# Splitting a recurrent layer's weights one stage early, into DRAM scratch

## The chip, the cores and the metric

One core of one Trainium2 chip runs the whole program. The metric is device time in microseconds (us) of one launch, the median of several runs. A profile shows one execution on the same chip; its span and its own time stand in the table below.

## The reference, cut to what matters

Two decoder layers over 512 tokens of 1024 channels, in float32. Layer 0 is attention, then a squared-ReLU MLP. Layer 1 is an RWKV-7 recurrent mixer, then another MLP. A final norm closes it. The recurrent mixer and the MLP:

```python
h = rmsnorm(h)
xx = shift(h) - h
xr, xw, xk, xv, xa, xg = [h + xx * mu[i] for i in range(6)]
r, k, v = xr @ w_r, xk @ w_k, xv @ w_v                  # 1024 x 1024 each
w = f(w0 + tanh(xw @ w1) @ w2)                          # rank 64
a = sigmoid(a0 + (xa @ a1) @ a2)                        # rank 64
g = sigmoid(xg @ g1) @ g2                               # rank 160
y = scan over 512 tokens of a 64 x 64 state per head, 16 heads
out = (groupnorm(y) + bonus(r, k, v)) * g @ w_o         # 1024 x 1024
mlp(h) = square(relu(h @ W1)) @ W2                      # W1 1024 x 4096
```

## The kernel before, in words

**Products in three passes.** A float32 operand x is split into a high half hi = x cast to fp32r and a low half lo = x - hi. A product is three TensorE passes, hi*hi, hi*lo and lo*hi (`mm3`, L187 to L190). So each weight chunk has to be loaded (SyncE issues a DMA into `wraw`, L177), cast by ScalarE into `whi` (L179), and subtracted by VectorE into `wlo` (L181) before TensorE may read it. `wraw` has three buffers, `whi` and `wlo` two each. A chunk is 128 x 2 x 512 elements, 512 KB, and feeds 24 matmuls of 128x128 by 512 columns in `gemm_group`.

**Order.** Outside of the scan a scheduler at build time orders the instructions of each engine. It places an instruction as soon as, by its own reckoning, the operands and the buffer are there; the order in the program decides between two that are ready. On the chip each engine, and each engine's DMA queue, then runs in that fixed order. In the scan the order of TensorE, ScalarE, VectorE and GpSimd is written out by hand (class `InOrder`); only the DMA issues are still placed by the scheduler.

**The stages of interest.** (1) The MLP of layer 0, here *MLP0*: 32 chunks of W1, 32 of W2, TensorE all the time. (2) The *LoRA stage* of the recurrent layer (`rwkv_layer`, L757 to about L960). `mix` makes the six inputs: per channel tile VectorE computes `mt` (L799), ScalarE casts it to `xh` (L804), and `xl` = mt - xh is made by GpSimd, or by VectorE for odd tiles of all but the first mix (`XLA`, L806). For the first mix, `xk`, VectorE also makes `h` and `xx` for each tile (L795, L797). `project` multiplies by half of w_k or w_r in four chunks; `wa_weights` and `g_weights` load and split the LoRA weights (L819 to L844, L902); `wa_first`, `wa_second`, `g_first`, `g_second` multiply. Results go to DRAM scratch through `spill`, issued from ScalarE's queue (L768), out of five buffers `sp`. (3) The *scan*: 16 units of work on 128 tokens by 4 heads. Beside them `beside` and `project_o` run the products by w_v, half of w_r, and w_o. Their 28 chunks come from `chunks`: the DMA at L1510, then quarter by quarter ScalarE's cast and GpSimd's subtraction (L1525, L1526; where the hand-written order is on, all lines read L149). SyncE also issues the scan's own small transfers, among them `kb` (L1125 to L1140), which TensorE transposes (`tkb`).

Of the kernel before, what the change touches and what calls it, by code (L numbers as in the profile page):

```python
# [10 lines left out]
F32 = mybir.dt.float32  # L11
# [55 lines left out]
XLA = 63  # L67
# [89 lines left out]
class Builder:  # L157
    def __init__(self, tc, A, out):
        self.tc, self.nc, self.A, self.out = tc, tc.nc, A, out
        self.uid = 0  # L160
        self.xq = None
        self.late = 0
        self.summed = None
# [21 lines left out]

    def mm3(self, ps, lh, ll, rh, rl, start, stop):
# [14 lines left out]
    def gemm_group(self, w, row0, nk, c0, xh, xl, evac, token_major=False, kc=2, prep=None, chunk=None,  # L201
                   banks=None, meanwhile=None):
# [4 lines left out]
        for kk in range(0, nk, kc):  # L207
            wh, wl = (chunk or self.wchunk)(w, row0 + kk, c0, kc)
            if prep is not None:
                for k in range(kc):  # L210
                    prep(kk + k)
            if kk == nk - kc and meanwhile is not None:
                meanwhile()
            for m in range(4):
                for k in range(kc):
                    a = kk + k
                    ms = slice(m * P, (m + 1) * P)
                    st, sp = a == 0, a == nk - 1
                    if token_major:
                        self.mm3(banks[m], xh[a][:, ms], xl[a][:, ms], wh[:, k, :], wl[:, k, :], st, sp)  # L220
                    else:
                        self.mm3(banks[m], wh[:, k, ms], wl[:, k, ms], xh[a], xl[a], st, sp)
                if kk + kc == nk:
                    evac(m, banks[m])

# [531 lines left out]
    def rwkv_layer(self):  # L757
        tc, nc, A = self.tc, self.nc, self.A
        W = {n: A["rwkv_" + n][0] for n in ("w_r", "w_k", "w_v", "w_o", "w0", "w1", "w2", "a0", "a1", "a2", "g1", "g2")}
# [7 lines left out]
        def spill(name, t, b, hf):  # L767
            nc.scalar.dma_start(scr[name][b * P:(b + 1) * P, hf * 512:(hf + 1) * 512], t)  # L768

        with ExitStack() as ctx:  # L770
# [38 lines left out]
            def raw(shape):  # L809
                return self.wp.tile(list(shape), F32, tag="wraw", name=self.nm("wraw"), bufs=3)  # L810
# [5 lines left out]
            def pair(src, tag, shape, bufs=1):  # L816
                hi, lo = small(tag + "h", shape, bufs), small(tag + "l", shape, bufs)
                nc.scalar.copy(hi, src)
                nc.vector.tensor_tensor(lo, src, hi, op=ALU.subtract)  # L819
                return hi, lo  # L820
# [7 lines left out]
            def wa_weights(w1, w2, w0):  # L828
                r1 = raw([P, KT, P])
                for o in (0, HD):  # L830
                    nc.sync.dma_start(r1[:, :, o:o + HD], w1.rearrange("(k p) c -> p k c", p=P))
                first = pair(r1, "l1", [P, KT, P])
                r2, bias = raw([P, D]), raw([P, D])
                nc.sync.dma_start(r2[0:HD], w2)
                nc.sync.dma_start(r2[HD:], w2)
                nc.sync.dma_start(bias[HD:HD + 1], w0.unsqueeze(0))
                nc.sync.dma_start(bias[96:97], w0.unsqueeze(0))
                hi, lo = small("l2h", [P, D]), small("l2l", [P, D])
                nc.scalar.copy(hi, r2)
                nc.vector.tensor_tensor(lo[0:HD], r2[0:HD], hi[0:HD], op=ALU.subtract)  # L840
                nc.vector.tensor_scalar(lo[HD:], r2[HD:], 0.0, None, op0=ALU.mult)
                nc.scalar.copy(lo[HD:HD + 1], bias[HD:HD + 1])
                nc.scalar.copy(lo[96:97], bias[96:97])
                nc.vector.tensor_tensor(lo[96:97], bias[96:97], lo[96:97], op=ALU.subtract)  # L844
                return first, (hi, lo)

            def wa_first(x, w, func):
# [5 lines left out]
                nc.vector.tensor_scalar(s2[HD:], f[HD:], 0.0, 1.0, op0=ALU.mult, op1=ALU.add)  # L853
# [18 lines left out]
            def project(w, x, hf, evac, behind=None):  # L872
                self.gemm_group(w, 0, KT, hf * 512, *x, lambda m, ps: evac(m, hf, ps), token_major=True,
                                chunk=behind and (lambda *a: self.wchunk(*a, behind=behind)))
# [11 lines left out]
            def g_weights():  # L886
                r1 = raw([P, KT, P])
                nc.sync.dma_start(r1, W["g1"][:, 0:P].rearrange("(k p) c -> p k c", p=P))
                g1 = pair(r1, "l1", [P, KT, P])
                r1 = raw([P, KT, P])  # L890
                for o in range(0, 96, 32):
                    nc.sync.dma_start(r1[:, :, o:o + 32], W["g1"][:, P:].rearrange("(k p) c -> p k c", p=P))
                t1 = pair(r1[:, :, 0:96], "g1", [P, KT, 96])
                r2 = raw([P, D])
                nc.sync.dma_start(r2, W["g2"][0:P, :])
                g2 = pair(r2, "l2", [P, D])
                r3 = raw([P, D])
                for o in range(0, 96, 32):
                    nc.sync.dma_start(r3[o:o + 32], W["g2"][P:, :])
                t2 = small("gst", [P, D])  # L900
                nc.scalar.copy(t2[0:96], r3[0:96])
                nc.vector.tensor_tensor(t2[64:96], r3[64:96], t2[64:96], op=ALU.subtract)  # L902
                return g1, t1, g2, t2
# [26 lines left out]
            project(W["w_k"], xk, 0, spilled("k"), self.ended)  # L930
            ww = wa_weights(W["w1"], W["w2"], W["w0"])
# [3 lines left out]
            project(W["w_k"], xk, 1, spilled("k"))  # L935
            xa = mix(4, 0)
            wa = wa_weights(W["a1"], W["a2"], W["a0"])
# [3 lines left out]
            project(W["w_r"], xr, 0, spilled("r"))  # L941
# [11 lines left out]
            with ExitStack() as cx:  # L953
# [531 lines left out]
                def evac_r(q):  # L1485
                    def evac(bk, ps):
                        t = self.tmp.tile([P, S], F32, tag="sq", name=self.nm("sq"))
                        nc.scalar.copy(t, ps)
                        nc.scalar.dma_start(tokens("r", q, bk), t.rearrange("p (m c) -> p m c", m=2))
                    return evac  # L1490

                def evac_v(q):
                    def evac(bk, ps):
# [3 lines left out]
                        nc.scalar.dma_start(tokens("v", q, bk), t.rearrange("p (m c) -> p m c", m=2))  # L1497
# [5 lines left out]
                        nc.scalar.dma_start(tokens("vc", q, bk), t.rearrange("p (m c) -> p m c", m=2))  # L1503
# [3 lines left out]
                def loads(todo):  # L1507
                    for w, k0, kc, c0, nc_ in todo:
                        raw = self.wp.tile([P, kc, nc_], F32, tag="wraw", name=self.nm("wraw"), bufs=3)
                        nc.sync.dma_start(raw, w[k0 * P:(k0 + kc) * P, c0:c0 + nc_].rearrange("(k p) c -> p k c", p=P))  # L1510
                        yield raw

                def chunks(todo):

                    ahead = loads(todo)
                    raws = [next(ahead)]
                    for w, k0, kc, c0, nc_ in todo:
                        raws.append(next(ahead, None))
                        raw = raws.pop(0)
                        hi = self.wp.tile([P, kc, nc_], F32R, tag="whi", name=self.nm("whi"))  # L1520
                        lo = self.wp.tile([P, kc, nc_], F32R, tag="wlo", name=self.nm("wlo"))
                        parts = [t.rearrange("p k c -> p (k c)") for t in (raw, hi, lo)]
# [31 lines left out]
                def project_o(cg, ks, ts, banks=None, last=True):  # L1554
# [5 lines left out]
                    for k0 in ks:  # L1560
# [5 lines left out]
                        for m in range(4):  # L1566
# [6 lines left out]
                            if last and k0 == ks[-1] and m % 2:  # L1573
                                for z in (0, 1):
# [7 lines left out]
                order = [(W["w_v"], xv, evac_v, 0), (W["w_v"], xv, evac_v, 1), (W["w_r"], xr, evac_r, 2), (W["w_r"], xr, evac_r, 3),  # L1582
                         (W["w_v"], xv, evac_v, 2), (W["w_v"], xv, evac_v, 3)]
                first_o, whole_o = (0, 2), (0, 2, 4, 6)
                weights = chunks([(w, kk, 4, q * CW, CW) for w, x, e, q in order for kk in (0, 4)]
                                 + [(W["w_o"], k0, 2, cg * 512, 512) for ks in (first_o, whole_o) for cg in range(2) for k0 in ks]
                                 + [(W["w_o"], k0, 2, cg * 512, 512) for k0 in (4, 6) for cg in range(2)])
# [70 lines left out]
    def mlp(self, layer, meanwhile=None):  # L1658
        tc, nc, A = self.tc, self.nc, self.A
        W1, W2 = A["mlp_w1"][layer], A["mlp_w2"][layer]  # L1660
        with ExitStack() as ctx:
            mp = ctx.enter_context(tc.tile_pool(name=f"mp{layer}", bufs=1))
            mw = ctx.enter_context(tc.tile_pool(name=f"mw{layer}", bufs=3))
            xh, xl = self.xtiles()
# [4 lines left out]
            for gcol in range(DFF // 512):  # L1669
# [6 lines left out]
                self.gemm_group(W1, 0, KT, gcol * 512, xh, xl, evac, prep=prep_x if gcol == 0 else None)  # L1676
# [8 lines left out]
            for gcol in range(2):  # L1685
# [13 lines left out]
                self.gemm_group(W2, 0, DFF // P, gcol * 512, mh, ml, evac, prep=prep)  # L1699
# [50 lines left out]
```

## Time and profile before

| | |
|---|---|
| median of 3 runs | 1502.92 us (1500.44 to 1506.06) |
| profiled execution, its own time | 1504.68 us |
| profiled execution, span | 1502.9 us |
| TensorE busy | 1421.1 us, 95% |
| VectorE, ScalarE, GpSimd busy | 890.4, 703.0, 351.1 us |
| moved by DMA | 163.97 MB, 109 GB/s over the span |

The span is the time between the first and the last instruction. Busy times of TensorE (PE) are modelled ends of pipelined matmuls; a matmul at the lower granted clock counts as busy too. A line number is that of the kernel; in the hand-ordered part all lines read L149, and the tiles tell the operations apart. `SPq` and `ACTq` rows are DMA issues by SyncE and ScalarE.

### The profile page before, as it was taken

What the parts mean: (1) busy time and instruction counts of PE and PEld (TensorE: products, weight loads), DVE (VectorE), ACT (ScalarE), POOL (GpSimd) and SP (SyncE); (2) the same over time, 40 slices, a digit from 0 to 9 for tenths busy, and PEclk for the clock granted to TensorE, in tenths of its full rate; (3) what the DMA queues carried; (4) which work ended last, traced back from release to release, by engine and by line L of the source; (5) the groups of instructions that cost most, each with busy time, mean ns of one, the idle gap of its engine ahead of it and who ended that gap; (6) DMA issues with size and microseconds to landing.
All of it is one profiled execution on the core that took longest, in us unless ns stands there. A gap on an engine that the chain in (4) does not pass through costs nothing. (4 is left out here: it accounts for less than half of the span.)

```text
span 1502.9 us, 24530 instructions
## 1 busy us (share of the span) xinstructions
PE 1421.1 (95%) x9506; PEld 1174.4 (78%) x9506; DVE 890.4 (59%) x1531; ACT 703.0 (47%) x1426; POOL 351.1 (23%) x368
## 2 busy tenths in 40 slices
PE   8999999999999999888988999989989999999998
PEld 6777777878888888666767888867778888888887
DVE  6456687723344464597767778888756233444543
ACT  4346675423333343346535666666645233333533
POOL 5111100300000010152255455556554000000100
PEclk9999999999999999899989999989999999999999
DMA  5343231423333233325654355443234333332321
GB/s 200 88 109 93 84 88 47 111 84 98 99 98 98 93 123 95 111 85 168 188 177 132 98 156 152 128 133 105 78 92 113 94 99 98 98 99 95 92 95 69
DMA packets 119677, 163.97 MB, mean 109 GB/s; under 512 B 23036, under 2 KB 58404, under 8 KB 119560
## 3 DMA queue, kind: packets, MB, share of 16 engines
q1 hardware_dynamic: 106824, 145.62, 33.0%
q10 hardware_dynamic: 12736, 16.78, 3.1%
q8 instruction: 75, 1.23, 0.4%
q14 instruction: 42, 0.34, 0.1%
HBM read 133.00 MB, written 19.92 MB: 102 GB/s over the span
## 5 line engine op out<-in xcount | busy, mean ns | idle before, releaser
L181 DVE TENSOR_TENSOR wlo<-wraw,whi 128x1024 fp32r<-128x1024 f32 x172 | 221.0, 1285 | 251.8 <-ACT whi L179 251.6
L179 ACT CAST whi<-wraw 128x1024 fp32r<-128x1024 f32 x172 | 180.4, 1049 | 223.6 <-PE g L189 184.9
L190 PE MATMUL g<-xh,wlo 128*128 128x512 f32 x512 | 199.1, 390 | 0.7 <-DVE wlo L181 0.6
L188 PE MATMUL g<-xh,whi 128*128 128x512 f32 x512 | 199.4, 390 | 0.0
L189 PE MATMUL g<-xl,whi 128*128 128x512 f32 x512 | 199.3, 389 | 0.0
L188 PE MATMUL g<-mh,whi 128*128 128x512 f32 x512 | 199.2, 389 | 0.0
L189 PE MATMUL g<-ml,whi 128*128 128x512 f32 x512 | 199.2, 389 | 0.0
L190 PE MATMUL g<-mh,wlo 128*128 128x512 f32 x512 | 199.2, 389 | 0.0
L366 POOL TENSOR_TENSOR acc<-acc,sq 128x512 f32<-128x512 f32 x29 | 49.4, 1704 | 610.5 <-issue 436.6
L196 DVE TENSOR_TENSOR ml<-m,mh 128x512 fp32r<-128x512 f32 x128 | 87.9, 689 | 151.2 <-ACT mh L195 151.2
L195 ACT CAST mh<-m 128x512 fp32r<-128x512 f32 x128 | 78.9, 618 | 190.1 <-PE g L190 189.9
L190 PEld LDWEIGHTS g<-xh,wlo 128*128 128x128 f32 x512 | 96.1, 188 | 21.2 <-DVE wlo L181 1.6
L188 PEld LDWEIGHTS g<-mh,whi 128*128 128x128 f32 x512 | 96.1, 188 | 20.1
L188 PEld LDWEIGHTS g<-xh,whi 128*128 128x128 f32 x512 | 96.1, 188 | 20.0 <-ACT rb L372 0.2
L190 PEld LDWEIGHTS g<-mh,wlo 128*128 128x128 f32 x512 | 96.1, 188 | 19.9
L189 PEld LDWEIGHTS g<-xl,whi 128*128 128x128 f32 x512 | 96.1, 188 | 19.9
L189 PEld LDWEIGHTS g<-ml,whi 128*128 128x128 f32 x512 | 96.1, 188 | 19.8
L149 POOL TENSOR_TENSOR wlo<-wraw,whi 128x256 fp32r<-128x256 f32 x100 | 76.9, 773 | 120.0 <-ACT whi L149 116.1
L806 POOL TENSOR_TENSOR xl<-mt,xh 128x512 fp32r<-128x512 f32 x28 | 47.8, 1722 | 86.6 <-ACT xh L804 79.9
L149 PE MATMUL side<-whi,xh 128*128 128x256 f32 x192 | 63.8, 332 | 0.0
L149 PE MATMUL g<-xh,whi 128*128 128x512 f32 x128 | 51.9, 406 | 5.8 <-DVE Qka L494 3.1
L149 PE MATMUL side<-wlo,xh 128*128 128x256 f32 x192 | 55.5, 289 | 1.8 <-POOL wlo L149 1.7
(331 smaller groups left out, 3065.7 us busy)
## 6 DMA issues: line engine op xcount, KB each, us to landing
wraw<-in_mlp_w_dram SPq DMA_DIRECT2D x128, 512.0 KB
wraw<-in_attn_w_in_dram SPq DMA_DIRECT2D x24, 512.0 KB
wraw<-in_rwkv_w_o_dram SPq DMA_DIRECT2D x16, 512.0 KB
wraw<-in_attn_w_out_dram SPq DMA_DIRECT2D x8, 512.0 KB
wraw<-in_rwkv_w_k_dram SPq DMA_DIRECT2D x8, 512.0 KB
wraw<-in_rwkv_w_r_dram SPq DMA_DIRECT2D x8, 512.0 KB
wraw<-in_rwkv_w_v_dram SPq DMA_DIRECT2D x8, 512.0 KB
xt<-in_x_dram ACTq DMA_DIRECT2D x4, 512.0 KB
```

Of the source, the lines that this page charges most:

```text
L149: ins = op(*args, **kw)
L179: ins = [nc.scalar.copy(hi, raw)]
L181: ins.append((eng or nc.vector).tensor_tensor(lo, raw, hi, op=ALU.subtract))
L188: mm(ps, lh, rh, start=start, stop=False)
L189: mm(ps, lh, rl, start=False, stop=False)
L190: mm(ps, ll, rh, start=False, stop=stop)
L195: nc.scalar.copy(hi, src)
L196: nc.vector.tensor_tensor(lo, src, hi, op=ALU.subtract)
L366: nc.gpsimd.tensor_tensor(self.acc[0], self.acc[0], sq, op=ALU.add)
L806: eng.tensor_tensor(xl[k], t, xh[k], op=ALU.subtract)
```

## The change

During MLP0 a new function `split_ahead` makes 40 jobs. Each job loads a piece of the recurrent layer's weights, splits it (ScalarE cast, VectorE subtraction) and writes both halves to DRAM scratch. `gemm_group` gets a hook `between`, called behind each chunk of MLP0, from which the jobs are put into the program, about two jobs per three chunks from the third of 64 chunks to the 59th. Their tiles `sraw`, `shi`, `slo` have two buffers each. In the recurrent layer `kept` loads the two halves with two DMAs (into `whi` and `wlo`, or every third time into two of the three `wraw` buffers), in place of load, cast and subtraction. `chunks` does the same for the scan, and the casts and subtractions there go. Besides, all `xl` are made by VectorE; `spill` and the scan's result writes are issued by SyncE, not ScalarE; two constant fills move from VectorE to GpSimd; the first w_k chunks are no longer ordered behind the end of MLP0.

```diff
+    def split_ahead(self, sp):
+        def keep(key, *parts):
+            for n, t in enumerate(parts):
+                d = nc.dram_tensor(self.nm("wsplit"), list(t.shape), F32).ap()
+                nc.sync.dma_start(d, t.bitcast(F32))
+                self.parts.setdefault(key, []).append(d)
+        def halves(key, raw):
+            hi, lo = tile_("shi"), tile_("slo")
+            n = raw.shape[-1]
+            nc.scalar.copy(hi[:, :n], raw)
+            nc.vector.tensor_tensor(lo[:, :n], raw, hi[:, :n], op=ALU.subtract)
+            keep(key, hi[:, :n], lo[:, :n])
+        def chunk(name, k0, kc, c0, n):
+            def job():
+                raw = tile_("sraw", F32)
+                nc.sync.dma_start(raw.rearrange("p (k c) -> p k c", k=kc),
+                                  W[name][k0 * P:(k0 + kc) * P, c0:c0 + n].rearrange("(k p) c -> p k c", p=P))
+                halves((name, k0, c0), raw)
+            return job
...
+        jobs = project("w_k", 0) + [first("w1", 2, 0, HD), second("w2", "w0")] + project("w_k", 1)
+        jobs += [first("a1", 2, 0, HD), second("a2", "a0")] + project("w_r", 0)
+        jobs += [first("g1", 1, 0, P), first("g1", 3, P, 32), gate_second, gate_rest]
+        for name, q in (("w_v", 0), ("w_v", 1), ("w_r", 2), ("w_r", 3), ("w_v", 2), ("w_v", 3)):
+            jobs += beside(name, q)
+        for cg in range(2):
+            jobs += project("w_o", cg)
+    def kept(self, key, kc, n):
+        self.turn3 = (self.turn3 + 1) % 3
+        tags = ("wraw", "wraw") if self.turn3 == 0 else ("whi", "wlo")
+        out = []
+        for tag, d in zip(tags, self.parts[key]):
+            t = self.wp.tile([P, kc, n], F32R, tag=tag, name=self.nm(tag), **({"bufs": 3} if tag == "wraw" else {}))
+            self.nc.sync.dma_start(t.rearrange("p k c -> p (k c)").bitcast(F32), d)
+            out.append(t)
+        return out
...
         def spill(name, t, b, hf):
-            nc.scalar.dma_start(scr[name][b * P:(b + 1) * P, hf * 512:(hf + 1) * 512], t)
+            nc.sync.dma_start(scr[name][b * P:(b + 1) * P, hf * 512:(hf + 1) * 512], t)
...
-                    eng = nc.vector if not first and (XLA >> i & 1) and k % 2 else nc.gpsimd
-                    eng.tensor_tensor(xl[k], t, xh[k], op=ALU.subtract)
+                    nc.vector.tensor_tensor(xl[k], t, xh[k], op=ALU.subtract)
...
-            project(W["w_k"], xk, 0, spilled("k"), self.ended)
-            ww = wa_weights(W["w1"], W["w2"], W["w0"])
+            project("w_k", xk, 0, spilled("k"))
+            ww = wa_weights("w")
...
-                        for i in range(4):
-                            r, h, l = (t[:, i * 256:(i + 1) * 256] for t in parts)
-                            nc.scalar.copy(h, r)
-                            nc.gpsimd.tensor_tensor(l, r, h, op=ALU.subtract)
-                            yield (hi, lo) if i == 3 else None
+                    for name, k0, kc, c0, n in todo:
+                        yield self.kept((name, k0, c0), kc, n)
...
+            def between():
+                nonlocal slots
+                slots += 1
+                while todo and (len(jobs) - len(todo)) * (total - 6) < (slots - 2) * len(jobs):
+                    todo.pop(0)()
```

## Rows read from the trace of the kernel before

**Rows 1.** The page, part 1: busy us, share and instructions by engine.

```profile
PE 1421.1 (95%) x9506; PEld 1174.4 (78%) x9506; DVE 890.4 (59%) x1531; ACT 703.0 (47%) x1426; POOL 351.1 (23%) x368
```

**Rows 2.** Busy time by stretch: bounds, length, busy by engine, granted clock, DMA share, GB/s.

```profile
268.00:630.00 362.00, 358.64 (x1603) 297.10 (x1602) 165.23 (x192) 132.76 (x183) 24.70 (x16) 1.00 0.34 100
632.00:671.00 39.00, 29.40 (x108) 22.41 (x108) 38.37 (x39) 15.87 (x23) 19.18 (x10) 0.83 0.25 69
632.00:773.00 141.00, 115.74 (x452) 87.81 (x452) 115.32 (x123) 72.24 (x114) 49.31 (x31) 0.89 0.46 142
773.00:1140.00 367.00, 337.11 (x4375) 290.11 (x4376) 274.80 (x659) 218.62 (x618) 207.31 (x263) 0.97 0.42 125
```

**Rows 3.** TensorE's waits, 600 to 820 us: waiter, releaser, total, times, longest.

```profile
PE l L868 <- DVE ls L855: 6.5, 2, 5.5
PE g L188 <- ACT xh L804: 4.7, 1, 4.7
PE g L189 <- DVE wlo L181: 4.3, 1, 4.3
```

**Rows 4.** VectorE's groups, 632 to 773 us: count, busy, mean ns, idle before.

```profile
L799 DVE SCALAR_TENSOR_TENSOR mt<-xx,mu,h 128x512 f32<-128x512 f32 x48 | 39.7, 870 | 0.0
L806 DVE TENSOR_TENSOR xl<-mt,xh 128x512 fp32r<-128x512 f32 x20 | 22.5, 1129 | 2.3 <-ACT xh L804 2.1
L181 DVE TENSOR_TENSOR wlo<-wraw,whi 128x1024 fp32r<-128x1024 f32 x10 | 14.4, 1436 | 11.2 <-ACT whi L179 11.2
```

**Rows 5.** GpSimd's largest group, 632 to 773 us.

```profile
L806 POOL TENSOR_TENSOR xl<-mt,xh 128x512 fp32r<-128x512 f32 x28 | 47.8, 1722 | 86.6 <-ACT xh L804 79.9 <-ACT xh L802 6.7
```

**Rows 6.** VectorE in order of time, first mix: start, us, operation, count.

```profile
633.72 1.28 DVE L797 TENSOR_TENSOR xx<-h 128x512 f32<-128x512 f32 x2
634.92 1.41 DVE L799 SCALAR_TENSOR_TENSOR mt<-xx,mu,h 128x512 f32<-128x512 f32 x2
...
638.59 2.36 DVE L797 TENSOR_TENSOR xx<-h 128x512 f32<-128x512 f32 x2
```

**Rows 7.** ScalarE and VectorE in MLP0, around one chunk, in order of time.

```profile
401.43 1.06 ACT L179 CAST whi<-wraw 128x1024 fp32r<-128x1024 f32 x1 [4.38 <-PE g L189]
402.52 1.23 DVE L181 TENSOR_TENSOR wlo<-wraw,whi 128x1024 fp32r<-128x1024 f32 x1 [4.21 <-ACT whi L179]
406.87 1.06 ACT L179 CAST whi<-wraw 128x1024 fp32r<-128x1024 f32 x1 [0.54 <-PE g L189]
```

**Rows 8.** Results of the LoRA products: ScalarE's evictions and their DMA issues.

```profile
L882 ACT ACTIVATE sp<-g x12: 585/598/602, 666.9 to 744.0; 128x512 f32<-128x512 f32 x12
L768 ACTq DMA_DIRECT2D scr_k<-sp x8: 326/327/354, 667.5 to 706.4; - x8
```

**Rows 9.** SyncE's DMA issues in order of time, the recurrent layer's constants.

```profile
273.28 0.34 SPq L745 DMA_DIRECT2D tri<-in_c_tri_dram  x1
```

**Rows 10.** DMA: two queues of the page's part 3, and the densest stretch (columns of Rows 2).

```profile
q1 hardware_dynamic: 106824, 145.62, 33.0%
q10 hardware_dynamic: 12736, 16.78, 3.1%
...
773.00:790.00 17.00, 16.30 (x111) 15.31 (x112) 10.69 (x18) 5.45 (x13) 12.22 (x15) 0.90 0.75 243
```

**Rows 11.** The scan's weight splits, 773 to 1140 us, GpSimd and ScalarE groups.

```profile
L149 POOL TENSOR_TENSOR wlo<-wraw,whi 128x256 fp32r<-128x256 f32 x99 | 76.2, 774 | 120.0 <-ACT whi L149 116.1 <-POOL lw L149 1.2 <-issue 1.1
...
L149 ACT CAST whi<-wraw 128x256 fp32r<-128x256 f32 x95 | 38.4, 406 | 2.5 <-PE side L149 2.0
```

**Rows 12.** TensorE's longest waits in the scan, 773 to 1140 us.

```profile
PE pxs L149 <- DVE x L149: 4.3, 7, 0.9
...
PE side L149 <- POOL wlo L149: 1.7, 3, 1.1
```

**Rows 13.** A transfer of one unit and TensorE's first use, in order of time.

```profile
914.13 0.59 SPq L1140 DMA_DIRECT2D kb<-la  x1
916.86 0.60 PE L149 MATMUL tkb<-ident,kb 128*128 128x128 f32 x4
```

More of the change, by code (lines that the diff above doesn't have):

```diff
@@ L201, in gemm_group @@
     def gemm_group(self, w, row0, nk, c0, xh, xl, evac, token_major=False, kc=2, prep=None, chunk=None,
[L202 removed]
+                   banks=None, meanwhile=None, between=None):
         if banks is None:
@@ L224, in gemm_group @@
                     evac(m, banks[m])
+            if between is not None:
+                between()
     def gemm_stream(self, jobs, kc=2):
@@ L814, in small, with kept @@
                 return pool_.tile(list(shape), F32R, tag=tag, name=self.nm(tag), bufs=bufs)
[L816 to L820, printed above, removed]
+            def kept(key, tag, shape):
+                out = []
+                for d, z in zip(self.parts[key], "hl"):
+                    t = small(tag + z, shape)
+                    nc.sync.dma_start((t.rearrange("p k c -> p (k c)") if len(shape) == 3 else t).bitcast(F32), d)
+                    out.append(t)
+                return out
             def lora1(x, w, m):
@@ L826, in lora1, with wa_weights @@
                 return ps
[L828 to L845, printed above, removed]
+            def wa_weights(n):
+                return kept((n + "1", 0), "l1", [P, KT, P]), kept(n + "2", "l2", [P, D])
             def wa_first(x, w, func):
@@ L886, in g_weights @@
             def g_weights():
[L887 to L899, printed above, removed]
+                g1, t1, g2 = kept(("g1", 0), "l1", [P, KT, P]), kept(("g1", P), "g1", [P, KT, 96]), kept("g2", "l2", [P, D])
                 t2 = small("gst", [P, D])
-                nc.scalar.copy(t2[0:96], r3[0:96])
-                nc.vector.tensor_tensor(t2[64:96], r3[64:96], t2[64:96], op=ALU.subtract)
+                nc.sync.dma_start(t2[0:96].bitcast(F32), self.parts["gst"][0])
                 return g1, t1, g2, t2
@@ L1502, in evac @@
                         nc.vector.tensor_tensor(hv(t), hv(ps), m.unsqueeze(2).broadcast_to([P, 8, HD]), op=ALU.subtract)
-                        nc.scalar.dma_start(tokens("vc", q, bk), t.rearrange("p (m c) -> p m c", m=2))
+                        nc.sync.dma_start(tokens("vc", q, bk), t.rearrange("p (m c) -> p m c", m=2))
                     return evac
[L1507 to L1511, printed above, removed]
-                def chunks(todo):
[L1515 to L1522, printed above, removed]
-                        for i in range(4):
-                            r, h, l = (t[:, i * 256:(i + 1) * 256] for t in parts)
-                            nc.scalar.copy(h, r)
-                            nc.gpsimd.tensor_tensor(l, r, h, op=ALU.subtract)
-                            yield (hi, lo) if i == 3 else None
+                def chunks(todo):
+                    for name, k0, kc, c0, n in todo:
+                        yield self.kept((name, k0, c0), kc, n)
                 def product(dst, ops, opens, closes):
@@ L1698, in evac @@
                     self.ended = self.sq_accum(k), added
-                self.gemm_group(W2, 0, DFF // P, gcol * 512, mh, ml, evac, prep=prep)
+                self.gemm_group(W2, 0, DFF // P, gcol * 512, mh, ml, evac, prep=prep, between=between)
+            assert not todo
             self.rstd = self.rstd_tokens(-0.5, pn)
```

82 lines of the change are left out of this document (64 added, 18 removed).

## The prediction

> **What bounds the kernel now.** I read the busy shares first: TensorE is busy 95% of the span, no other engine more than 59% [rows 1]. So a gain can come only from TensorE's idle time and from matmuls run at the lower clock. The table by stretch says where these are [rows 2]. MLP0 (268 to 630 us) has TensorE busy 358.6 of 362 us at clock 1.00: nothing to win, only to lose. The LoRA stage (632 to 773 us) has 115.7 busy of 141 us at a mean granted clock of 0.89. The scan with its tail (773 to 1140 us) has 337.1 of 367 us at 0.97.
>
> How much of the LoRA stage is work? The code gives 448 matmuls of 512 columns: 12 projection chunks x 24 = 288, four LoRA first products x 24 = 96, the second products 2 x 16 + 32 = 64. The stretch counts 452, four of the scan's among them [rows 2]. At full clock one takes 5.44 / 24 = 0.227 us: the cast of the next chunk, which waits for TensorE each time, comes 5.44 us after the one before (401.43, 406.87) and a chunk is 24 matmuls [rows 7]. That is 101.5 us of work in 141 us.
>
> What holds it up? Over its first 39 us VectorE is busy 38.4 us and TensorE only 29.4 at clock 0.83 [rows 2]; TensorE's largest waits are for VectorE's LoRA operands, for `xh` and for a `wlo` [rows 3]. So VectorE sets the pace at first; later short waits and the clock that falls after them do.
>
> **The change part by part.**
>
> *LoRA stage, VectorE.* GpSimd's 28 `xl` take 47.8 us [rows 5], and while they run VectorE is slower: two `xx` took 1.28 us before the first of them and 2.36 us beside them [rows 6]. Over the stage 48 `mt` took 39.7 us where 48 x 0.705 = 33.8 was due, 20 `xl` 22.5 where the undisturbed two-input operation gives 20 x 0.64 = 12.8 [rows 4, 6]: 15.6 us lost in these two groups alone. The change removes that, and the `wlo` (14.4 us, [rows 4]), and adds 28 x 0.64 = 17.9 us. VectorE goes from 115.3 to at most 115.3 - 15.6 - 14.4 + 17.9 = 103 us, less the LoRA splits, which I don't price. The first mix now is `h`, `xx`, `mt`, `xl` per tile, 0.705 + 0.64 + 0.705 + 0.64 = 2.69 us, 21.5 us for eight. It starts at 632.4, so ends near 654; TensorE's first group needs 21.8 us and follows tile by tile, ending a chunk later, near 660. Before, its first eviction was at 666.9 [rows 8] and the last about 3 us later: some 10 us come from here. Behind it 101.5 - 21.8 = 79.7 us of matmuls remain, with VectorE no longer ahead of them. I leave 8 us for the waits of the second products on `ls` and the like, which the change does not touch [rows 3], and 5 us for the lower clock behind them: 660 + 79.7 + 13 = 753 instead of 773. **-20 us.** Ends: -35 us if only the first 4.4 us and the 101.5 us of work remain; the other end comes from the DMAs. The stage must move 12.6 MB of halves for the chunks, 7.5 MB for the LoRA weights, 9.4 MB of results, 2.1 MB of `h`: 31.6 MB. The densest 17 us of the trace moved 243 GB/s [rows 10]; at that rate 130 us, so -11 us; and if the wait for halves simply takes VectorE's place, 0. I take -20, since 243 GB/s came at a DMA share of only 0.75.
>
> *MLP0, the new work.* A job costs ScalarE one cast, VectorE one subtraction, as in the chunk rows 1.06 and 1.23 us [rows 7]. 40 jobs add 42 and 49 us to engines that are busy 132.8 and 165.2 of 362 us [rows 2], so there is room; what counts is whether a job delays a chunk's own pair. That pair is ready 2.32 us after TensorE frees the buffers and needed after 5.44; the slack of 3.1 us covers one job's cast and subtraction (2.29 us). Price 0, plus 0.1 us per job for meetings with the squares and `ml`: **+4 us.** Without that cover each job would cost up to 2.29 us, 92 us in all.
>
> *MLP0, the DMAs.* The stretch moves 100 GB/s x 362 us = 36 MB now. The jobs load 20.7 MB (32 chunks x 0.524 and the LoRA weights) and write 41.0 MB: 98 MB. By the page the loading queue used 33.0% of 1502.9 us for 145.62 MB, 3.4 us per MB, ScalarE's queue, all of it writes after the first 2 MB, 2.8 us per MB [rows 10]: 57 x 3.4 + 41 x 2.8 = 309 us, in the 322 us (59 chunks) in which the jobs are laid out. It fits, at over nine tenths of the DMA engines. Will the chunk loads be late? They are issued when a `wraw` buffer comes free, three chunks (16 us) ahead of their cast, less the 2.3 us of the split: 14 us for a load that has up to six job transfers (3.1 MB, 10 us) ahead of it. It fits too. Ends: 0, and +42 us, if 243 GB/s is the ceiling (98 / 0.243 = 404 us).
>
> *SyncE's queue.* Every job puts a load and two writes on SyncE, and a write waits for ScalarE and VectorE; behind a waiting write stand MLP0's own loads. In program order that would be bad. But the issues are not in program order: the constants of the recurrent layer stand behind MLP0's eighth chunk, near 311 us, and were issued at 273.3 [rows 9]. Writes are placed when the scheduler expects their data, loads when a buffer frees. I cost it at nothing.
>
> *Scan.* 107 casts by ScalarE (38.4 us for 95) and 111 subtractions by GpSimd (76.2 us for 99) leave [rows 11]. But TensorE waited for `wlo` only 1.7 us there; its longest named wait is 4.3 us for VectorE's `x`, a step of the recurrence [rows 12]. The removed operations stand in the hand-written order ahead of others and, as in rows 6, slow VectorE. Of the 30 us of idle and about 10 us of lower clock [rows 2] I credit 9. Against that each of the 28 chunks now moves 1.05 MB instead of 0.52, 1.8 us more at 3.4 us per MB, on the queue of the scan's own transfers; a `kb` is used 2.7 us after its issue [rows 13], so there is little slack. Where such a load is ahead, TensorE waits; about a quarter of 16 units, with some 1.3 us, costs 5. **-4 us.** Ends: -25 and, if each of 16 units lost 1.8 us, +29.
>
> What the row says of GpSimd's neighbour is a slowdown by 1.08 us for two operations [rows 6]. The Trainium skill, SBUF — State Buffer, "Who interferes with whom", has a stricter rule: a VectorE instruction with two SBUF inputs and a GpSimd instruction that reads SBUF exclude each other for the whole instruction. By that rule the 76.2 us taken off GpSimd in the scan would free more of VectorE than I credit, and the scan would stand at its lower end, -25 us, the third rival below. Rows 4 and 5 bear out only a part: 15.6 us lost in two groups beside 47.8 us of GpSimd.
>
> *Spills by SyncE.* ScalarE saves 0.33 us per issue [rows 8], not on TensorE's path; SyncE has the time. Fills moved to GpSimd: under 1 us each, free.
>
> **The sum.** -20 + 4 - 4 = -20 us on the profiled execution's 1504.7 us gives 1484.7. The median of the runs is 1.8 us below that execution: **1483 us.**
>
> **The rivals.**
>
> 1. *The DMA engines are the bound of MLP0* (slower). Place: the chunk loads of MLP0, behind job traffic. It decides once loads land later than 14 us after their issue, that is once the mix of reads and writes runs below about 300 GB/s. For it: 98 MB; no stretch of the trace did better than 243 GB/s. Against it: its share was 0.75 there. Price: +42 in MLP0, LoRA stage -11, scan 0: 1502.9 + 31 = 1534 us; half of it gives about 1515.
>
> 2. *The DMAs give the gain back later* (no change). The scan's transfers wait behind twice the weights, +14 us, half of its upper end, in place of -4: 1501 us. Or the spills do it: now on the loads' queue, they wait behind chunk halves, and five `sp` buffers serve eight results. If three results of each of three second products wait for a chunk (1.05 MB, 4.3 us at 243 GB/s, shared by the three), that is 13 us: 1496 us. The Trainium skill, DMA: Bandwidth & Descriptors, "Queues, rings and completion order", says that a DMA engine takes turns between queues; by that the spills lose their own turn by the move. No row here shows it.
>
> 3. *The scan gains its whole lower end*, -25: -20 + 4 - 25 = -41, 1462 us. For it: 76 us off GpSimd. Against it: the small named waits [rows 12].
>
> **How the numbers follow.** Forecast 0.56 (its own range 1470 to 1494), rival 1 0.14, rival 2 0.22, rival 3 0.08. For eight times in ten the range goes from 1460 to 1517: it leaves out the worse half of rival 1 and little on each side else. A difference under 0.5% (7.5 us) can't be told from none. Faster: 0.56 + 0.08 and a fifth of rival 2, 0.68; within 0.5%: most of rival 2, 0.17; slower: rival 1 and a little, 0.15.
>
> **What would show it.** In the table by stretch: the LoRA stage near 120 us with VectorE under 100 us and GpSimd next to nothing; `mt` near 0.71 us. MLP0 within 5 us of 362, TensorE at clock 1.00, with the DMA share from 0.34 to over 0.8. Chunk casts in MLP0 that wait for DMA, not for TensorE, would mean rival 1. TensorE's waits on `kb` in the scan would mean rival 2. I am wrong altogether if the LoRA stage stays over 135 us with VectorE idle: then VectorE was not what held it.

## The result and the profile after

The changed kernel takes 1482.72 us (median of 4 runs, 1481.37 to 1486.55) against 1503.01 of the kernel before beside it: ratio 0.9868, 95% interval 0.9842 to 0.9894. The forecast was 1483. The total is right; the parts are not. MLP0 lost three times what was priced; the scan gained three times what was credited, the LoRA stage gained a little more than forecast, and these errors nearly cancel.

The stages are cut here by rows of each trace: MLP0 from its first W1 matmul to the first `h` of the first mix, the LoRA stage from there to the scan's first `pc` matmul, the scan from there to its last `h`, and the rest to the end of the span.

| us | W1 starts | MLP0 | LoRA stage | scan | rest | span |
|---|---|---|---|---|---|---|
| before | 273.0 | 359.4 | 133.9 | 372.6 | 364.0 | 1502.9 |
| after | 273.5 | 372.6 | 110.1 | 360.4 | 363.9 | 1480.5 |
| difference | +0.5 | +13.2 | -23.8 | -12.2 | -0.1 | -22.4 |

The page, part 1 and the two large queues of part 3 (q1 is SyncE's, q10 ScalarE's), of the kernel after [rows 1, 10]:

```profile
PE 1411.7 (95%) x9506; PEld 1169.5 (79%) x9506; DVE 876.3 (59%) x1575; ACT 685.3 (46%) x1334; POOL 219.2 (15%) x232
...
q1 hardware_dynamic: 140264, 246.56, 51.7%
q10 hardware_dynamic: 2112, 2.10, 0.4%
```

GpSimd gives up 132 us. SyncE's queue moves 101 MB more, 15 of them results that ScalarE's queue carried before. TensorE is busy 9 us less in a span that is 22 us shorter. Now by stretch, first the kernel after (columns of [rows 2]), then the kernel before between the same bounds:

```profile
268.00:646.00 378.00, 365.79 (x1610) 300.74 (x1608) 215.08 (x234) 173.88 (x228) 25.76 (x19) 0.98 0.80 269
646.00:756.00 110.00, 99.65 (x424) 78.80 (x424) 76.80 (x121) 47.71 (x85) 0.52 (x1) 0.95 0.65 231
756.00:1117.00 361.00, 339.36 (x4397) 293.03 (x4398) 251.43 (x665) 183.97 (x511) 123.76 (x153) 0.97 0.53 166
```

```profile
632.00:766.00 134.00, 109.86 (x432) 83.56 (x433) 112.45 (x119) 71.29 (x112) 47.80 (x28) 0.89 0.44 135
766.00:1139.00 373.00, 341.99 (x4392) 293.56 (x4391) 276.66 (x663) 218.56 (x619) 208.82 (x265) 0.96 0.43 128
```

In the LoRA stage VectorE falls from 112.5 to 76.8 us and the mean granted clock rises from 0.89 to 0.95. In the scan VectorE does as many instructions in 25 us less. From 268 to 646 us TensorE idles 12.2 of 378 us, at a mean clock of 0.98.

VectorE's two largest groups in the LoRA stage of the kernel after (count, busy us, mean ns, idle before), to be held against [rows 4]:

```profile
L896 DVE SCALAR_TENSOR_TENSOR mt<-xx,mu,h 128x512 f32<-128x512 f32 x48 | 34.8, 745 | 0.2
L902 DVE TENSOR_TENSOR xl<-mt,xh 128x512 fp32r<-128x512 f32 x48 | 32.2, 685 | 7.1 <-PE g L285 3.8 <-ACT xh L901 3.1
```

`mt` went from 870 to 745 ns, `xl` from 1129 to 685. The first eviction of a result comes 23.6 us after the first `h` (669.7 less 646.1); before it was 34.5 [rows 8].

What took 13.2 us in MLP0? TensorE's waits there, of the kernel after (waiter, releaser, total, times, longest), and below them its only wait in MLP0 of the kernel before:

```profile
PE g L286 <- DVE wlo L181: 6.4, 3, 3.8
PE g L504 <- POOL msr L498: 3.6, 2, 1.9
PE g L284 <- DVE res L1755: 1.1, 1, 1.1
PE g L284 <- ACT whi L179: 0.6, 1, 0.6
```

```profile
PE g L406 <- POOL msr L400: 4.0, 2, 2.3
```

Counted matmul by matmul against the kernel before, 7.3 of the 13.2 us are lost by 303 us and 4.9 between 545 and 572 us: stalls, and matmuls at the lower clock behind the first of them.

The longest wait in order of time, same kernel (start, us, operation, idle before and releaser):

```profile
283.10 1.04 ACT L205 CAST shi<-sraw 128x1024 fp32r<-128x1024 f32 x1
284.05 1.99 ACT L179 CAST whi<-wraw 128x1024 fp32r<-128x1024 f32 x2
284.71 3.80 DVE L206 TENSOR_TENSOR slo<-sraw,shi 128x1024 fp32r<-128x1024 f32 x2
...
288.43 2.35 DVE L181 TENSOR_TENSOR wlo<-wraw,whi 128x1024 fp32r<-128x1024 f32 x2
...
289.70 0.79 PE L286 MATMUL g<-xh,wlo 128*128 128x512 f32 x1 [3.83 <-DVE wlo L181]
```

A job's cast stands ahead of two chunk casts, and two job subtractions (`slo`) ahead of the two `wlo` that TensorE waits for. The two took 3.80 us, the first and a part of the second beside work of GpSimd. After the stall the mean granted clock is 0.53 from 289 to 295 us and 1.00 from 295 to 301. The second place is at 543 us, SyncE's queue and then ScalarE in order of time:

```profile
531.38 0.32 SPq L199 DMA_DIRECT2D wsplit<-shi  x1
534.37 0.38 SPq L177 DMA_DIRECT2D wraw<-in_mlp_w_dram  x1
534.81 0.46 SPq L199 DMA_DIRECT2D wsplit<-slo  x1
535.32 0.42 SPq L212 DMA_DIRECT2D sraw<-in_rwkv_w_o_dram  x1
```

```profile
542.86 1.05 ACT L205 CAST shi<-sraw 128x1024 fp32r<-128x1024 f32 x1 [6.84 <-issue]
543.81 0.62 ACT L291 CAST mh<-m 128x512 fp32r<-128x512 f32 x1
...
544.33 1.05 ACT L179 CAST whi<-wraw 128x1024 fp32r<-128x1024 f32 x1
```

On SyncE nothing is issued for some 3 us, until the last `wlo` frees a `wraw` at 534.35; the job's write and load stand behind that. ScalarE then reaches the job's cast and idles 6.84 us, with the chunk's `mh` and `whi` behind it. The row names no releaser; the load issued at 535.32 is the one I take it to wait for.

### The profile page after: what moved, and what is told of

Its sections match the earlier page's. It is cut to its first block, busy times and chain, and to the rows that moved or that the text cites. A ratio compares the mean times of both kernels' runs of the same rounds, so it can differ in the third digit from the quotient of the medians.

```text
span 1480.5 us, 24724 instructions
## 1 busy us (share of the span) xinstructions
PE 1411.7 (95%) x9506; PEld 1169.5 (79%) x9506; DVE 876.3 (59%) x1575; ACT 685.3 (46%) x1334; POOL 219.2 (15%) x232
## 3 DMA queue, kind: packets, MB, share of 16 engines
q8 instruction: 75, 1.23, 0.4%
## 4 chain that ended last, share of the span: by engine, by line
PE 66%; DVE 5%; DMA 4%; ACT 2%; issue 2%; POOL 0%; SPq 0%; ACTq 0%; DVEq 0%; POOLq 0%
PE g L286 15%; PE g L284 15%; PE g L285 15%; PE side L148 6%; PE prod L148 2%; PE pxs L148 2%; PE psc L148 2%; DMA sraw<-in_rwkv_w_v_dram 1%; DMA sraw<-in_rwkv_w_o_dram 1%; DVE wlo L181 1%; DMA kb<-la 1%; PE py L148 1%; PE val L148 1%; PE pc L148 1%; PE g L490 1%
## 5 line engine op out<-in xcount | busy, mean ns | idle before, releaser
L181 DVE TENSOR_TENSOR wlo<-wraw,whi 128x1024 fp32r<-128x1024 f32 x160 | 203.9, 1275 | 201.6 <-ACT whi L179 201.5
L179 ACT CAST whi<-wraw 128x1024 fp32r<-128x1024 f32 x160 | 167.6, 1048 | 190.0 <-PE g L285 152.1
L285 PE MATMUL g<-xl,whi 128*128 128x512 f32 x512 | 200.1, 391 | 0.0
L206 DVE TENSOR_TENSOR slo<-sraw,shi 128x1024 fp32r<-128x1024 f32 (+1 forms) x37 | 46.3, 1254 | 47.2 <-ACT shi L205 47.0
L205 ACT CAST shi<-sraw 128x1024 fp32r<-128x1024 f32 (+1 forms) x37 | 38.6, 1044 | 54.0 <-DMA sraw<-in_rwkv_w_o_dram 12.1
L1734 DVE TENSOR_TENSOR m<-m 128x512 f32<-128x512 f32 x64 | 43.6, 687 | 13.8 <-ACT m L1733 13.8
L148 PE MATMUL g<-xl,whi 128*128 128x512 f32 x128 | 51.0, 398 | 0.0
```

The lines of the kernel that those rows point to most:

```text
L148: ins = op(*args, **kw)
L179: ins = [nc.scalar.copy(hi, raw)]
L181: ins.append((eng or nc.vector).tensor_tensor(lo, raw, hi, op=ALU.subtract))
L205: nc.scalar.copy(hi[:, :n], raw)
L206: nc.vector.tensor_tensor(lo[:, :n], raw, hi[:, :n], op=ALU.subtract)
L1734: nc.vector.tensor_tensor(t, t, t, op=ALU.mult)
```

## The experiments

All were timed beside the kernel before. The stages are those of one profiled execution each:

| us | W1 starts | MLP0 | LoRA stage | scan | time, ratio to before (95%) |
|---|---|---|---|---|---|
| e1 no jobs | 273.7 | 362.1 | 111.3 | 359.6 | 1471.01, 0.9777 (0.9750 to 0.9803) |
| e2 before + jobs | 275.0 | 371.5 | 133.7 | 371.2 | 1516.70, 1.0079 (1.0057 to 1.0102) |
| e3 jobs tied | 270.8 | 359.1 | 110.1 | 360.8 | 1466.59, 0.9756 (0.9724 to 0.9788) |
| e4 xl on GpSimd | 270.9 | 372.3 | 135.2 | 361.0 | 1507.07, 1.0023 (1.0008 to 1.0039) |
| e5 before, xl moved | 273.3 | 359.4 | 125.8 | 374.2 | 1501.40, 0.9987 (0.9972 to 1.0003) |
| e6 scan splits | 272.0 | 364.3 | 110.8 | 378.3 | 1493.04, 0.9926 (0.9908 to 0.9944) |
| e7 spills by ScalarE | 274.3 | 373.2 | 109.2 | 365.9 | 1487.44, 0.9890 (0.9870 to 0.9910) |
| e8 jobs unwritten | 271.3 | 374.6 | 110.7 | 362.9 | 1485.54, 0.9876 (0.9857 to 0.9895) |
| e9 tied + GpSimd | 274.9 | 359.1 | 110.9 | 364.9 | 1479.91, 0.9832 (0.9809 to 0.9856) |
| e10 tied + ScalarE | 276.0 | 360.4 | 111.1 | 362.0 | 1472.38, 0.9778 (0.9751 to 0.9804) |
| e11 subtraction tied | 271.9 | 368.4 | 110.5 | 359.2 | 1476.47, 0.9810 (0.9788 to 0.9833) |
| e12 tied + both | 274.8 | 360.7 | 110.1 | 378.8 | 1488.93, 0.9892 (0.9872 to 0.9912) |

The start of W1 wanders between 270.8 and 276.0 us, also among e3, e9, e10 and e12, which have the same jobs and the same MLP0. So I compare stages, and take nothing from a start.

**e1, e2: is MLP0's loss the jobs, and nothing else?** e1 leaves one job of 40; e2 puts the 40 into the kernel before, unused.

```diff
# e1
-        return jobs
+        return jobs[:1]
# e2 (in mlp of the kernel before)
+            if layer == 0:
+                jobs = self.split_ahead(...)
```

> The changed kernel with one job of 40 left; every read of halves takes that job's two halves, so the recurrent layer reads as many bytes but the wrong weights, and 39 pieces are never split. If the sum is right (MLP0 pays 13.7 us for the jobs, the LoRA stage and the scan gain 23.8 and 12.2 us), MLP0 goes back to about 364 us between its first us and the first mix, the other stages stay within 2 us of the changed kernel, and the time is near 1469 us (ratio to the kernel before 0.978). Rival: the gain of the scan comes from somewhere else or the later stages read faster when the halves are in one place: then LoRA stage or scan move by more than 3 us.

> The kernel before with the 40 jobs added to MLP0 and their halves never read. Price of the jobs alone: 13.7 us if they cost only MLP0, so near 1516.5 us (ratio 1.009), MLP0 378 us. Rival: the price depends on what follows (the tail of the queue runs into the recurrent layer): then it is more, up to 1525 us, or under 1508 us if the changed schedule behind MLP0 caused part of the loss.

Both times came as expected (the 378 us expected of e2 are counted from 268 us). The jobs cost 12.1 us in MLP0 of the kernel before (371.5 less 359.4) and 10.5 us in the changed one (372.6 less 362.1), and change the other stages by at most 1.4 us. With the one job that is left 2.7 of the 13.2 us stay, 1.5 of them a wait for `wlo`; e3 below keeps every other edit of the change and doesn't lose them.

**e3: order or bandwidth?** The job's cast and subtraction are ordered behind the cast and subtraction of the neighbouring chunk. Bytes, work and buffers stay.

```diff
+        self.pair = ins
...
-            nc.scalar.copy(hi[:, :n], raw)
-            nc.vector.tensor_tensor(lo[:, :n], raw, hi[:, :n], op=ALU.subtract)
+            self.after(nc.scalar.copy(hi[:, :n], raw), self.pair[0])
+            self.after(nc.vector.tensor_tensor(lo[:, :n], raw, hi[:, :n], op=ALU.subtract), self.pair[1])
```

> The changed kernel, each job's cast and subtraction ordered (no wait, issue order only) behind the cast and subtraction of the chunk it stands next to. Order theory (the 13.7 us come from job casts and subtractions that stand in ScalarE's and VectorE's fixed order ahead of chunk pairs, bunched at the start of MLP0 and near 545 to 560 us): the stalls of 3.8 us near 286 us and 2.2 us near 561 us go, MLP0 is at 366 to 370 us, the time 1472 to 1476 us. Bandwidth theory (98 MB at a share of 0.80 of the DMA engines make the loads late): the same bytes in the same stretch, so no change, 1480 to 1486 us, or worse, since a cast then waits for its load with the next chunk behind it.

MLP0 is back at 359.1 us, with all 40 jobs, and the time is below the 1472 to 1476 of the order theory. Its stretch and all of TensorE's waits from 262 to 640 us, of e3:

```profile
268.00:630.00 362.00, 357.67 (x1597) 295.96 (x1596) 210.62 (x230) 170.21 (x223) 23.43 (x18) 1.00 0.82 279
```

```profile
PE g L285 <- ACT xh L902: 4.7, 1, 4.7
PE g L505 <- POOL msr L499: 3.6, 2, 1.9
```

The DMA engines moved 279 GB/s at a share of 0.82, more per us than in the kernel after, and TensorE waits for no `wlo`. The order was the cause; the bytes cost TensorE nothing. This is the fastest version, 1466.59 us; its interval lies wholly below that of the changed kernel. The same tied jobs gave 359.1 to 360.7 us again in e9, e10 and e12.

What stood in the wrong order shows in ScalarE's waits before job casts from 273 us to the end of MLP0; the largest row of the kernel after, then the only one of e3:

```profile
ACT shi L205 <- DMA sraw<-in_rwkv_w_o_dram: 12.1, 3, 8.0
```

```profile
ACT shi L206 <- DMA sraw<-in_rwkv_w_k_dram: 0.6, 1, 0.6
```

Over all such rows ScalarE stood 50 us in front of job casts whose load had not landed, in e3 0.6 us. So a job's cast ahead of a chunk's cast costs not only its own 1.05 us but also the wait for its load. TensorE lost 13 us in all, so most of that wait fell into time that ScalarE had to spare.

**e8: do the writes matter?** Only the first job's halves are written.

```diff
         def keep(key, *parts):
+            if key != ("w_k", 0, 0):
+                return
```

> The changed kernel, all 40 jobs with their loads, casts and subtractions, but only the first job's halves are written to scratch and every later read takes those (38.5 of 41 MB of writes left out; the result is not the reference's for that). Order theory: the first MLP's loss of 13.7 us comes from job casts and subtractions ahead of chunk pairs, so it stays: first mix at 643 to 648, time 1479 to 1485. If the writes are the cause, by their DMA time or because a buffer is free only after its write, it falls to that of one job: first mix at 635.8 to 638, time 1471 to 1474.

MLP0 stays at 374.6 us, at a DMA share of 0.51 and with waits for `wlo` again:

```profile
268.00:646.00 378.00, 364.79 (x1600) 298.02 (x1598) 214.65 (x232) 171.52 (x226) 25.56 (x19) 0.98 0.51 160
```

```profile
PE g L294 <- DVE wlo L181: 5.4, 4, 3.6
PE g L292 <- ACT m L1741: 3.8, 3, 1.6
```

A loss of this size needs neither the 38.5 MB of writes nor their place on SyncE's queue. But it isn't made at the same places: without writes the jobs come earlier (13 job casts from 380 to 422 us, against 6 subtractions of jobs there in the kernel after), and 8.0 us are lost from 381 to 431 us and nothing behind. So e8 says nothing of the place at 543 us, where the late load at 535.32 is one link.

**e11: cast or subtraction?** e3 without the tie on the job's casts.

```diff
-            self.after(nc.scalar.copy(hi[:, :n], raw), self.pair[0])
+            nc.scalar.copy(hi[:, :n], raw)
```

> e3 with only the job's subtraction ordered behind the neighbouring chunk's own subtraction; the job's casts are placed by the scheduler again. The stalls of the changed kernel's first MLP were 7.4 us behind VectorE's wlo and some 1.6 us behind ScalarE, so I expect that the subtraction carries most: first mix at 630 to 635, time 1468 (1465 to 1472). If the casts in front of whi are the cause (the subtraction comes late since its cast did): first mix at 640 to 646 and 1476 to 1482.

A miss; the band of the casts held (first mix at 640.3 us). MLP0 takes 368.4 us: the tied subtraction wins 4.2 us of the 13.5 between the kernel after and e3, the tie of the cast on top of it the other 9.3 (the cast's tie alone was not run). TensorE's wait is booked on `wlo`, which VectorE makes, but most is lost on ScalarE, as here in e11:

```profile
292.05 1.05 ACT L206 CAST shi<-sraw 128x1024 fp32r<-128x1024 f32 x1 [8.29 <-DMA sraw<-in_rwkv_w_k_dram]
293.00 1.05 ACT L179 CAST whi<-wraw 128x1024 fp32r<-128x1024 f32 x1
```

The chunk's `whi` stands behind a job's cast that waited 8.29 us for its load. Such waits sum to 67 us in MLP0 of e11.

**e4, e5: what won the LoRA stage?** e4 is the changed kernel with `xl` on GpSimd as it was; e5 the kernel before with `xl` on VectorE alone.

```diff
# e4
-                    nc.vector.tensor_tensor(xl[k], t, xh[k], op=ALU.subtract)
+                    eng = nc.vector if not first and k % 2 else nc.gpsimd
+                    eng.tensor_tensor(xl[k], t, xh[k], op=ALU.subtract)
# e5: the reverse, in the kernel before
```

> The changed kernel with the low halves xl made as before (all of the first mix and the even tiles of the others on GpSimd). If VectorE beside GpSimd was what held the LoRA stage, this part alone gives back a good half of its 24 us: the stage from 110 to 122 to 128 us, time 1494 to 1500 us. Rival: the splits that left (wlo and the LoRA weights, 26 us of VectorE) made the gain, and xl on GpSimd now hides beside it: stage at most 115 us, time 1483 to 1488 us.

> The kernel before, with all xl made by VectorE and nothing else changed: weights are still split in the recurrent layer. With xl left on GpSimd the changed kernel lost its whole gain in the LoRA stage (135.2 us against 110.1). If the shared port alone is the cause (theory A), moving xl alone gives nearly all of it: LoRA stage 112 to 116 us, time about 1483. If VectorE's sum decides (theory B), it goes from 115.3 - 15.6 + 17.9 = 118 us of work with the wlo still in it, TensorE cannot be faster than that, and some waits for wlo remain: LoRA stage 122 to 128 us, time about 1494. I expect B: 1494 (1486 to 1500). Scan 372.6 +- 1.5 as before.

With the splits gone but `xl` on GpSimd nothing is won: 135.2 us, more than the 122 to 128 expected. VectorE has room (80.3 us busy of 135), but its groups of e4 show what it waits for:

```profile
L896 DVE SCALAR_TENSOR_TENSOR mt<-xx,mu,h 128x512 f32<-128x512 f32 x48 | 42.1, 910 | 22.6 <-POOL xl L903 22.3
```

22.3 us of waiting for GpSimd's `xl`, and `mt` at 910 ns. With `xl` moved but the splits kept (e5) the stage takes 125.8 us, in theory B's band; the total can't be told from the kernel before, where B said 1494, and why is open. The stretch of e5, with nothing on GpSimd:

```profile
632.00:758.00 126.00, 107.40 (x425) 82.84 (x424) 101.57 (x145) 71.62 (x112) 0.00 (x0) 0.89 0.45 141
```

The first eviction divides the stage:

| us | to the first eviction | behind it |
|---|---|---|
| before | 34.5 | 99.4 |
| e4 (splits gone) | 34.6 | 100.6 |
| e5 (xl moved) | 26.0 | 99.8 |
| after (both) | 23.6 | 86.5 |

The first mix is won by moving `xl`. The 13 us behind it came only with both. (e5 also lacks the smaller edits of the change; of these only the spills were tested alone, in e7.)

**e6: is the scan's gain the splits?** The scan splits its 28 chunks again; 20 jobs are left.

> The changed kernel, but the scan splits its own 28 chunks again (load, ScalarE cast, GpSimd subtraction); only the 20 jobs of the LoRA stage are left in the first MLP. Theory: the scan's gain of 12.2 us comes from these casts and subtractions; then the scan goes back from 360.4 to about 372 us. The first MLP has half the jobs, so it loses about half of its 13.7 us; LoRA stage 110 as in the changed kernel. Sum 1482.7 + 11.5 - 7 = 1487 (1482 to 1492). Rival: the scan gains by something else (spills by SyncE, no work left over from the LoRA stage); then it stays at 361 us and the time is about 1476.

The scan goes to 378.3 us, so the splits are the cause and the rival falls. That it is 5.7 us more than before, and the time 1 us above the range, I can't explain; e12 below, whose added work waits for no load, is as far above it.

**e7: the spills.** In `spill`, `evac_r` and `evac_v`:

```diff
-            nc.sync.dma_start(scr[name]...
+            nc.scalar.dma_start(scr[name]...
```

> The changed kernel with the spills and the scan's result writes issued by ScalarE's queue again. The prediction priced the move at nothing: then 1482.7 +- 2.5, LoRA stage 110 +- 1.5, scan 360 +- 2. Its second rival says that spills behind the weight halves cost up to 13 us: then moving them back gains, LoRA stage 100 to 106 and 1470 to 1478. A single wait of 5.3 us in the scan for the reload of a spilled tile should go in that case.

The LoRA stage is 0.9 us shorter, the scan 5.5 us longer, outside the 360 +- 2 expected. Moving the spills back wins nothing, so they weren't a cost behind the chunk halves; whether the move to SyncE gained is open, for the intervals of the two kernels overlap. The new wait of 5.3 us for `lw<-scr_w`, just ahead of the scan's first matmul and so counted in the LoRA stage, is in both, so the queue of the spills does not make it.

**e9, e10, e12: which part of the scan's splits?** To e3's scan is added, at the places of the old quarter splits and on constant tiles, GpSimd's subtraction alone (e9), ScalarE's cast alone (e10), or a cast with the subtraction waiting for it (e12, shown here).

```diff
-                        yield self.kept((name, k0, c0), kc, n)
+                        out = self.kept((name, k0, c0), kc, n)
+                        for i in range(4):
+                            nc.scalar.copy(self.dm[0], self.msk[:, :256])
+                            nc.gpsimd.tensor_tensor(self.dm[1], self.msk[:, :256], self.dm[0], op=ALU.subtract)
+                            yield out if i == 3 else None
```

> e3 (jobs ordered behind the chunk pairs, scan 360.8 us) with one thing put into the scan: where the kernel before had a quarter of a chunk's split, GpSimd makes a 128x256 subtraction on a constant tile that nothing reads (112 in all, some 76 us of GpSimd); no cast, and no wait on it. Theory: the scan's gain comes from VectorE beside a quieter GpSimd (VectorE busy 276.7 us before, 251.4 after, for the same operations); then VectorE goes back to 270 to 276 us in the scan, the scan to 369 to 373 us, the time to 1476 (1473 to 1480). Rival, that ScalarE's casts or the waits on the split held the scan: scan 360 to 363 and 1467.

> e3 with 112 casts of 128x256 by ScalarE in the scan in place of e9's subtractions, on a constant tile (some 38 us of ScalarE), nothing on GpSimd. Theory (the GpSimd neighbour is the cause): scan within 2.5 us of 360.8, time 1467 (1465 to 1470). Rival, ScalarE's place in the hand-written order: scan 366 to 373, time 1472 to 1479.

> e3 with both put into the scan: where the kernel before split a quarter of a chunk, ScalarE casts 128x256 of a constant tile and GpSimd subtracts that cast from it (112 of each); nothing reads the result and no load stands before it. e9 (GpSimd alone) made the scan 4.1 us longer than e3's 360.8, e10 (ScalarE alone) 1.2 us; before to after were 12.2. If the two add up and the rest of the 12.2 is waiting on the chunk's load or TensorE's waiting on the split: scan 365 to 367, VectorE 270 to 276 us. If GpSimd's wait for ScalarE in the hand-written order is the rest: scan 370 to 374. I lean to the first (0.6). Time: MLP of layer 0 as in e3 (359 us from its first matmul), so 1471 to 1474 by the first, 1476 to 1480 by the second, plus up to 5 us where that MLP starts later, as in e9 and e10.

The scan's stretch of e3, e9, e10 and e12, one fence each, VectorE's busy time the third:

```profile
740.00:1101.00 361.00, 340.83 (x4397) 294.04 (x4398) 250.80 (x664) 183.76 (x511) 123.77 (x153) 0.96 0.52 165
```

```profile
745.00:1110.00 365.00, 340.82 (x4396) 293.77 (x4397) 267.15 (x664) 184.14 (x511) 194.56 (x265) 0.97 0.51 164
```

```profile
747.00:1110.00 363.00, 340.05 (x4398) 293.01 (x4399) 251.37 (x666) 217.77 (x618) 123.45 (x153) 0.97 0.52 165
```

```profile
746.00:1124.00 378.00, 342.31 (x4396) 294.06 (x4396) 277.98 (x661) 218.66 (x621) 208.20 (x265) 0.97 0.50 158
```

GpSimd's subtractions alone slow VectorE by 16 us and the scan by 4.1: neither band of e9 held. ScalarE's casts alone come to 1.2 us, which is inside the spread of the six scans without added work (359.2 to 362.9 us: the kernel after, e1, e3, e4, e8, e11). Together, with the one waiting for the other, the scan is 18.0 us longer, as with the real splits of e6 (17.5). I had leaned to a sum of 5; that failed, and so did the upper band, which ended at 374. No load stands before e12's casts and TensorE waits for none of its results, so waiting for chunks isn't what the splits cost. GpSimd's group of e12:

```profile
L148 POOL TENSOR_TENSOR dm<-msk,dm 128x256 f32<-128x256 f32 x100 | 76.0, 760 | 126.7 <-ACT dm L148 118.6 <-DMA kb<-la 4.4 <-DMA scr_v<-sq 2.2
```

GpSimd stands 118.6 us waiting for ScalarE, with the scan's own GpSimd steps behind, as it did 116.1 us before [rows 11]. That is not more idle time, though: by the stretches above GpSimd idles 170 us in e9 as in e12, in e9 mostly behind VectorE. What grows from e9 to e12 is VectorE's busy time, 267 to 278 us (276.7 before), and TensorE's waits for VectorE, 17 to 24 us in sum (11 in e3); none of TensorE's waits is for GpSimd. So it is shown that the chained pair costs far more than its halves. Whether it does so because GpSimd's own steps come late or because its subtractions fall more on VectorE's work is not shown.

Two reserves. e9's subtraction is the lighter one: it reads one tile twice and takes 0.62 us in the median, e12's 0.73. And e12 has one buffer for the cast, so ScalarE also waits for GpSimd, 23.2 us by its waits against 2.3 before. How much of the 18 us that adds is open.

## Why the prediction was right, and where it wasn't

That the total came out at 1483 us is luck: MLP0 came 9.2 us worse than forecast, the LoRA stage and the scan together 12.0 us better.

**LoRA stage, -20: right in place, somewhat small (-23.8).** The first mix gave 10.9 us where "some 10" was said. Behind it 12.9 came instead of 10. Mis-sized was the loss beside GpSimd: 15.6 us in two groups. e5, with GpSimd silent and the splits kept, has VectorE at 101.6 us in its stage instead of 112.5, with 28 more `xl` of 0.686 us (19.2 us) in it: 30 us lost beside GpSimd, twice my figure, for the rows I had added up left out `xx`, `h` and the splits. The DMA end didn't come: 231 GB/s over 110 us are 25 MB, where the prediction had 31.6 MB in the stage.

**MLP0, +4: wrong (+13.2).** The step that failed is "the slack of 3.1 us covers one job's cast and subtraction (2.29 us)". It took one job ahead of a chunk's pair, with its load landed. In the trace two job subtractions stand together ahead of two `wlo` (284.71 to 288.43) and take 3.80 instead of 2.46 us; and ScalarE stands 50 us of MLP0 at job casts whose load has not landed, up to 8.0 us at one, for which the sum had no term. The prediction said itself that issues are not in program order, and used it for SyncE's good [rows 9]; the same holds for ScalarE and VectorE, where it harms. The DMA step held: e3 moves 279 GB/s and TensorE waits for no chunk. "I cost it at nothing" for SyncE's queue is not fully right (534.37), but with all 40 jobs on that queue e3 loses nothing.

**Scan, -4: wrong (-12.2).** The whole gain was credited at 9 us before the loads. The term that was mis-sized is the split itself: chained as in the kernel before, cast and subtraction cost 18.0 us (e12) where the subtraction alone cost 4.1 and the cast alone 1.2. By which path the chain costs it is open, as said. I read [rows 12], small TensorE waits for `wlo`, as a bound on the gain; but TensorE's waits for VectorE in the scan fell from 20 to 13 us in sum when the splits went, so those rows hold only the last link of each delay. The price of the chunk loads was too high: TensorE waited for `kb` 1.8 us, not 5.

The Trainium skill, SBUF — State Buffer, "Who interferes with whom", states an exclusive lock of the shared port; in e9 71 us more of GpSimd (194.6 less 123.8) lengthened VectorE's work by 16.4 us (267.2 less 250.8). That is an average, and does not show whether single instructions exclude each other. The scan's lower end of -25, which the rule suggested, did not come.

**Rivals.** 1 (DMA bound in MLP0): refuted by e3 and e8. 2 (DMAs give the gain back): refuted by the scan of the kernel after and by e7. 3 (scan at -25): the gain was half of it. None of the three held MLP0's real loss, job work ahead of chunk work. Rival 1 also rested on a wrong reading, "no stretch of the trace did better than 243 GB/s": the kernel before moved more in other 17 us (columns of [rows 2]).

```profile
3.00:20.00 17.00, 13.37 (x59) 11.14 (x60) 12.30 (x17) 8.73 (x13) 8.47 (x7) 1.00 0.86 303
765.00:782.00 17.00, 15.23 (x75) 12.72 (x74) 11.97 (x20) 3.02 (x9) 10.51 (x13) 0.80 0.86 273
```

The row given as the densest [rows 10] was not, so 243 GB/s was no ceiling, and the upper ends worked out from it had no ground in the trace.

**The signs.** `mt` near 0.71 us (0.745), VectorE under 100 us (76.8), GpSimd next to nothing (0.5), DMA share up to 0.80: as said. The LoRA stage near 120 us: better, 110. MLP0 within 5 us at clock 1.00: not, 13.2 us at 0.98.

## What to carry to other kernels

Work moved under a saturated stage needs an explicit place behind the stage's own work on every in-order engine: here a scheduler that places what it reckons ready put it in front, and room in the busy share didn't protect the critical pair. A step that stands ahead in a fixed order costs its work and the wait for its own load. The tie gave back all 13 us. And where one engine makes an operand for another inside a hand-ordered chain, removing the pair can be worth more than both halves: price it as a pair, not only by the work of each.

## What was not expected of the hardware

- The DMA engines moved 296 GB/s at a share of 0.88 over 239 us of MLP0 (301 to 540 us, kernel after); the kernel before came to 303 GB/s at 0.86 only over 17 us (3 to 20 us).
- A job's subtraction of 128x1024 took 1.21 to 1.23 us wherever GpSimd was idle. Of the two at 284.71 the first, beside GpSimd's `acc` and then a cast all along, took 2.30 us, the second, beside that cast for 0.5 us, 1.57. Two that overlapped other GpSimd work, a fill at 303.76 and a 128x4 step at 325.67, by 0.5 and 1.0 us took 1.23: these two did not slow it.
- After a stall of 3.83 us TensorE ran at the lower clock for about 5 us (mean granted clock 0.53 from 289 to 295 us): matmuls 0.63 us long from 290.29 to 294.13, 0.40 us from 294.85.
